# First weight pieces in quarters, gate folds one per unit, block-sum transfers and block sums of x later

## The chip, the cores and the metric

The kernel runs on one core of a Trainium2 chip. The metric is the time of one execution on the device, in microseconds (us). Five engines work side by side: TensorE (PE in the profile, with its weight loads as PEld), VectorE (DVE), ScalarE (ACT), GpSimd (POOL) and SyncE (SP). Here SP only issues DMA transfers; POOL does a little arithmetic and also issues transfers.

## What is computed

The reference is one block of an encoder on 512 positions of 1024 channels, in float32:

```python
h = rmsnorm(x, w)                       # 512 x 1024
parts = h @ w_in                        # one combined projection, 10240 columns
# branch A: Re(2-D DFT) of 4 channel groups, * silu(z_A), linear map to 1024
# branch B, 4 heads of 512 channels:
xc = silu(centred_dwconv(xm, 5 taps) + bias)
q, k = block_diag_proj(xc, ...); v = block_diag_proj(xm, ...)   # blocks of 4 channels
i_pre, f_pre = linear maps of (q, k, v) to one number per head and direction
hh = mlstm(q, k, v, i_pre, log_sigmoid(f_pre))   # forward and backward scans, summed
u = (rmsnorm(sigmoid(o) * hh) + skip * xc) * silu(z_B)          # linear map to 1024
y = sigmoid(g_A) * y_A + sigmoid(g_B) * y_B
out = final_rmsnorm(x + y @ w_out)
```

Three pieces matter here: the projection, the input and forget gates of branch B, which need q, k and v of all heads, and the norm inside u.

## The kernel before

**Products in three.** Every large product is made of three matmuls. `mm3` (L94) splits each operand into a high part, rounded to a shorter format, and a low part, the rest: L96 takes high times high, L97 and L98 the two cross products. `hi_of` (L86) makes high parts on ACT, `lo_of` (L89) low parts on DVE. So each piece of weights costs one step on ACT and one on DVE before TensorE can take it.

**Units.** Weights come in units of 128 x 1024 numbers (512 KB). `fetch` issues a unit's load on SP into one of three raw buffers (L130). `prepare` (L141 to L152) splits it into `whi` and `wlo`, of which there are two buffers each, and issues the next fetch as soon as the raw buffer is free. A unit gives 24 matmuls of 128x512 in `proj`.

**The start.** `load_x` (L203) loads one of eight tiles of x, transposed, and splits it into `hhi` (ACT) and `hlo` (DVE, L206). The first three units are loaded and split in pieces by `load_part` (L209), between the tiles of x: in halves of 512 columns, with the tiles 0 and 4. ACT then squares the tiles of x (L249), DVE adds them (L252), and `norm_rows` (L305) sums over the channels with small matmuls (L309) and makes the norm factor rc; `norm_bcast` (L313) spreads it.

**The loop over units.** One z unit, then 16 x units. The product of each is evacuated and scaled by the norm on DVE (L352) as a tile `sa`; from the fifth on, `conv` (L323) makes one convolved tile `sb` a unit, with four steps on DVE (L331) and two on ACT (L328, L333). At unit 6 `load_gates` (L266) issues six loads of 256 KB with the gate weights, into the tile buffers sa1 to sb3, whose x tiles come later. At unit 10 `fold_gates` (L273) folds the block-diagonal weights into them: for each of the six pieces a multiplication (L282) and a reduction (L283) on DVE. A sum (L285) and a copy make the gate matrix of it. From then on `gate_mm` (L293) multiplies it with the x tiles, one matmul for `sa` and one for `sb` of each (L299), in float32 and with an output of 32 rows; `tile_position` puts four of them in turn on four groups of TensorE's columns. All add up in one accumulator.

**The gates and the heads.** `gate_chain` (L405) copies the accumulator with ACT (L410) and picks rows of it with two small matmuls (L417). Then the four heads follow. Each makes queries, scores (`wf` tiles, cut by POOL's affine selects at L510 and L513), value products (L614, from weights that POOL makes at L494), and products with the output gate (L543 to L545). At the end of a head ACT makes sums of squares (L632), POOL the norm factor `rr` from them (L634, L635), DVE scales by it (L636), and TensorE transposes (L646). ACT scales the convolved tiles by the skip weights (L641).

**Block sums.** The last linear maps use products of block sums in the manner of Strassen. The sums of weight blocks are made in DRAM by 20 jobs: SP copies a block (L158), and POOL adds another to it with an accumulating transfer (L162), which waits for the copy and for earlier sums. The program places the jobs between its stages (`next_job`). SP's transfers are kept in the order of the program, POOL's L162 are not. Sums of blocks of x are made by `block_sums` (L664): four calls, each with two loads on POOL (L668) and work on DVE and ACT, at units 0 to 3 of the first loop behind the heads (L681); at units 6 and 7 of that loop ACT evacuates the products (L697).

**The order of the work.** A scheduler puts the instructions of each engine in order ahead of time, by a model of when each can start. `pin` takes an instruction out of that: it keeps its place of the program among the pinned ones of its engine.

Of the kernel before, what the change touches and what calls it, by code (L numbers as in the profile page):

```python
# [11 lines left out]
ALU = mybir.AluOpType  # L12
# [14 lines left out]
SSQ_AT, RB_AT = (2, 2), (2, 6)  # L27
LOAD_AT, FOLD_AT, CONV_AT, DRAIN_AT = 6, 10, 4, 12
Z_FIRST = 3
# [10 lines left out]
def hybrid_block(ctx: ExitStack, tc, xT, xn, units, blocks, vecs, gates, gbias, consts, dft, fnw, out):  # L40
# [115 lines left out]
    def sum_job(i):  # L156
        if i < 4 * NB:
            pin(nc.sync.dma_start(sums[i // 4, i % 4], blocks[i // 4, (2, 0, 0, 1)[i % 4]], max_dma_last_dim=4 * S * 4))  # L158
        if i > 0:
            b, k = (i - 1) // 4, (i - 1) % 4  # L160
            src = (blocks[b, 3], sums[b, 0], blocks[b, 2], sums[b, 1])[k]
            gp.dma_start(sums[b, k], src, accum_op=ALU.add, max_dma_last_dim=4 * S * 4)  # L162

# [45 lines left out]
    def load_part(i, n):  # L209
        if n == 0:  # L210
            raws[i] = tl("raw", [P, 1024], bufs=NRAW)
            if i < 2:
                items.append((tl("whi", [P, 1024], F32R, bufs=2), tl("wlo", [P, 1024], F32R, bufs=2)))
            else:
                items.append((tl("so0", [P, 1024], F32R), tl("so1", [P, 1024], F32R)))
        hs = slice(n * S, (n + 1) * S)
        nc.sync.dma_start(raws[i][:, hs], units[i][:, hs])
        hi_of(items[i][0][:, hs], raws[i][:, hs])
        lo_of(items[i][1][:, hs], raws[i][:, hs], items[i][0][:, hs])

    state["raw"] = state["split"] = NU0
    for k in range(8):
        load_x(k)
        if k % 4 == 0:
            for i in range(NU0):
                load_part(i, k // 4)
    for i in range(NU0):
# [12 lines left out]
    def wview(name):  # L240
        return vc[:, name : name + 64].rearrange("p (i d) -> p i d", i=16)
# [24 lines left out]
    def load_gates():  # L266
        for n, t in enumerate(("sa1", "sa2", "sa3", "sb1", "sb2", "sb3")):
            j, half = n // 2, n % 2
            grep[j, half] = tl(t, [P, 8, 16, 4])
            src = gates[:, j, 8 * half : 8 * half + 8].rearrange("p i (g d) -> p i g d", d=4)  # L270
            pin(nc.sync.dma_start(grep[j, half], src))

    def fold_gates():  # L273
        folded.append(True)
        folds = [tl("sa0", [P, 2, 16, 16]), tl("sb0", [P, 1, 16, 16])]
        for j, off in enumerate((V_WQ, V_WK, V_WV)):
            dst = folds[j // 2][:, j % 2]
            for half in range(2):
                hs = slice(8 * half, 8 * half + 8)
                g = grep[j, half]  # L280
                w = wview(off)[:, hs].unsqueeze(2).to_broadcast([P, 8, 16, 4])
                ve.tensor_tensor(out=g, in0=g, in1=w, op=ALU.mult)  # L282
                ve.tensor_reduce(out=dst[:, hs, :], in_=g, axis=AX.X, op=ALU.add)  # L283
        f = folds[0]
        ve.tensor_tensor(out=w_gate[0][:, :, 0:16], in0=f[:, 0], in1=f[:, 1], op=ALU.add)  # L285
        se.activation(w_gate[1][:, :, 0:16], folds[1][:, 0], AF.Copy)

# [80 lines left out]
    for n, (kind, i) in enumerate([("z", 0)] + [("x", i) for i in XO]):  # L368
# [17 lines left out]
        if n == LOAD_AT:  # L386
            load_gates()
        if n == FOLD_AT and not folded:
            fold_gates()
        if n >= CONV_AT and ready:  # L390
            conv(ready.pop(0))
        while n >= DRAIN_AT and ready:
            conv(ready.pop(0))
        if folded and len(pending) >= 5:
            gate_mm([pending.pop(0) for _ in range(4)])
# [285 lines left out]
    for q in range(2):  # L681
        accs = [bank("acc") for _ in range(4)]
        for n in range(8):
            if q == 0 and n < 4:
                block_sums(n)
            if q == 1 and n == 2:
# [445 lines left out]
```

## Time and profile before

| | |
|---|---|
| median of 3 runs | 772.92 us (771.41 to 774.53) |
| the profiled execution | 773.64 us |
| its span, first to last instruction | 771.9 us |
| TensorE's granted clock | 0.999 |
| PE busy | 758.5 us (98%) |
| DVE busy | 526.4 us (68%) |
| ACT busy | 411.5 us (53%) |
| POOL busy | 70.5 us (9%) |

The times in the views are counted from the start of the span. In a row of the timeline stand start, duration, engine, line, operation, out<-in, and in brackets how long the engine was idle before it and who ended that. In the view of stretches, each engine's busy time stands with its count of instructions behind it, in the order PE, PEld, DVE, ACT, POOL, then clock, DMA share and GB/s. Matmuls overlap, so a row's duration is longer than the step from one start to the next.

### The profile page before, as it was taken

What the parts mean: (1) busy time and instruction counts of PE and PEld (TensorE: products, weight loads), DVE (VectorE), ACT (ScalarE), POOL (GpSimd) and SP (SyncE); (2) the same over time, 40 slices, a digit from 0 to 9 for tenths busy, and PEclk for the clock granted to TensorE, in tenths of its full rate; (3) what the DMA queues carried; (4) which work ended last, traced back from release to release, by engine and by line L of the source; (5) the groups of instructions that cost most, each with busy time, mean ns of one, the idle gap of its engine ahead of it and who ended that gap; (6) DMA issues with size and microseconds to landing.
All of it is one profiled execution on the core that took longest, in us unless ns stands there. A gap on an engine that the chain in (4) does not pass through costs nothing.

```text
span 771.9 us, 10941 instructions
## 1 busy us (share of the span) xinstructions
PE 758.5 (98%) x4146; PEld 642.1 (83%) x4146; DVE 526.4 (68%) x813; ACT 411.5 (53%) x643; POOL 70.5 (9%) x147
## 2 busy tenths in 40 slices
PE   8999999999999999999999999999999999999996
PEld 7876776788788888888888887899999999988885
DVE  6599876676758574767475693247667678557875
ACT  7434445659446843685463443156544577643444
POOL 0100001011310310031101210000010100000002
PEclk9999999999999999999999999999999999999999
DMA  8348658639460984197403565267654456554452
GB/s 273 105 148 260 190 138 237 173 134 259 97 192 28 289 213 125 43 302 217 120 27 137 141 221 157 86 181 225 192 164 147 135 157 198 179 183 140 147 193 109
DMA packets 40949, 128.55 MB, mean 167 GB/s; under 512 B 4801, under 2 KB 5314, under 8 KB 35778
## 3 DMA queue, kind: packets, MB, share of 16 engines
q1 hardware_dynamic: 37378, 104.80, 40.5%
q0 software_dynamic: 3520, 23.07, 15.2%
q8 instruction: 32, 0.52, 0.3%
q14 instruction: 19, 0.16, 0.1%
HBM read 125.76 MB, written 44.04 MB: 220 GB/s over the span
## 4 chain that ended last, share of the span: by engine, by line
PE 87%; DVE 5%; DMA 3%; ACT 2%; issue 1%; POOL 1%; SPq 0%; POOLq 0%; ACTq 0%
PE acc L96 16%; PE acc L98 16%; PE acc L97 16%; PE wk L98 7%; PE wk L96 7%; PE wk L97 7%; PE acc L544 3%; PE acc L545 3%; PE acc L543 3%; DMA sum<-in_blocks_dram 2%; PE wk L299 1%; PE wk L614 1%; DMA raw<-in_units_dram 1%; DVE t2k L331 1%; DVE wlo L89 1%
## 5 line engine op out<-in xcount | busy, mean ns | idle before, releaser
L89 DVE TENSOR_TENSOR wlo<-raw,whi 128x1024 fp32r<-128x1024 f32 (+1 forms) x105 | 125.4, 1196 | 82.5 <-ACT whi L86 82.4
L86 ACT ACTIVATE whi<-raw 128x1024 fp32r<-128x1024 f32 (+1 forms) x105 | 108.8, 1039 | 128.4 <-PE acc L97 92.0
L96 PE MATMUL acc<-hhi,whi 128*128 128x512 f32 x248 | 97.0, 395 | 2.6 <-ACT whi L86 2.6
L98 PE MATMUL acc<-hhi,wlo 128*128 128x512 f32 x248 | 97.2, 393 | 0.0
L97 PE MATMUL acc<-hlo,whi 128*128 128x512 f32 x248 | 97.0, 391 | 0.0
L96 PEld LDWEIGHTS acc<-hhi,whi 128*128 128x128 f32 x248 | 46.5, 188 | 15.0 <-ACT whi L86 4.8
L98 PEld LDWEIGHTS acc<-hhi,wlo 128*128 128x128 f32 x248 | 46.5, 188 | 14.7 <-DVE sa L352 2.5
L89 DVE TENSOR_TENSOR gwl<-raw,gwh 128x1024 fp32r<-128x1024 f32 (+1 forms) x39 | 47.1, 1208 | 17.0 <-ACT gwh L86 17.0
L86 ACT ACTIVATE gwh<-raw 128x1024 fp32r<-128x1024 f32 (+1 forms) x39 | 40.9, 1048 | 29.7 <-PE acc L97 10.8
L97 PEld LDWEIGHTS acc<-hlo,whi 128*128 128x128 f32 x248 | 46.6, 188 | 10.1 <-DVE hlo L206 0.7
L545 PE MATMUL acc<-whi,hlo 128*128 128x512 f32 x128 | 50.5, 394 | 0.0
L544 PE MATMUL acc<-wlo,hhi 128*128 128x512 f32 x128 | 50.4, 393 | 0.0
L97 PE MATMUL acc<-sb,whi 128*128 128x512 f32 x128 | 50.2, 392 | 0.0
L96 PE MATMUL acc<-sa,whi 128*128 128x512 f32 x128 | 49.8, 390 | 0.3 <-ACT whi L86 0.3
L97 PE MATMUL wk<-vlo,phi 128*128 128x512 f32 x128 | 49.8, 389 | 0.0
L96 PE MATMUL wk<-vhi,phi 128*128 128x512 f32 x128 | 49.6, 390 | 0.0
L98 PE MATMUL acc<-sa,wlo 128*128 128x512 f32 x128 | 49.0, 391 | 0.5 <-DVE wlo L89 0.5
L98 PE MATMUL wk<-vhi,plo 128*128 128x512 f32 x128 | 48.0, 389 | 0.0
L543 PE MATMUL acc<-whi,hhi 128*128 128x512 f32 x128 | 47.6, 392 | 0.0
L331 DVE SCALAR_TENSOR_TENSOR t2k<-sa,vecs,t2k 128x510 f32<-128x510 f32 (+1 forms) x64 | 45.9, 743 | 0.5
L98 PEld LDWEIGHTS acc<-sa,wlo 128*128 128x128 f32 x128 | 24.0, 188 | 5.8 <-DVE wlo L89 1.0
L96 PEld LDWEIGHTS wk<-vhi,phi 128*128 128x128 f32 x128 | 24.0, 188 | 5.7 <-PE acc L417 0.8
(399 smaller groups left out, 1909.4 us busy)
## 6 DMA issues: line engine op xcount, KB each, us to landing
raw<-in_units_dram SPq DMA_DIRECT2D x69, 512.0 KB, 3.9
sum<-in_blocks_dram SPq DMA_DIRECT2D x20, 1024.0 KB, 7.8
raw<-sum SPq DMA_DIRECT2D x64, 256.0 KB, 3.6
raw<-in_blocks_dram SPq DMA_DIRECT2D x48, 256.0 KB, 3.6
sum<-in_blocks_dram POOLq DMA_DIRECT2D x10, 1024.0 KB, 10.9
sum<-sum POOLq DMA_DIRECT2D x10, 1024.0 KB, 9.6
raw<-sum SPq DMA_DIRECT2D x8, 512.0 KB, 4.5
raw<-in_blocks_dram SPq DMA_DIRECT2D x6, 512.0 KB, 4.1
```

Source lines behind the costliest of these rows:

```text
L86: se.activation(dst, src, AF.Copy, scale=scale)
L89: ve.tensor_tensor(out=dst, in0=src, in1=hi.bitcast(F32), op=ALU.subtract)
L96: pin(te.matmul(acc, wh, xh, start=start, stop=False, **skip), pinned)
L97: te.matmul(acc, wh, xl, start=False, stop=False, **skip)
L98: te.matmul(acc, wl, xh, start=False, stop=stop, **skip)
L299: te.matmul(gate_ps[rows, :], w_gate[j][:, i, :], r, start=p < 2, stop=p >= 14, tile_position=(0, 32 * (2 * b + j)))
L331: ve.scalar_tensor_tensor(out=cv[:, o], in0=src[:, s], scalar=cw[k], in1=cv[:, o], op0=ALU.mult, op1=ALU.add)
L543: te.matmul(ops[t], hv(x_hi, k)[:, ts], wh[:, ks], start=k == 0, stop=False)
L544: te.matmul(ops[t], hv(x_hi, k)[:, ts], wl[:, ks], start=False, stop=False)
L545: te.matmul(ops[t], hv(x_lo, k)[:, ts], wh[:, ks], start=False, stop=k == 7)
L614: te.matmul(vp[:, ds], xm[c0 + d][:, b * P : (b + 1) * P], vbf[:, d, :], start=True, stop=True)
```

## The change

Four things are changed, and nothing of what is computed.

1. The first three units come in quarters of 256 columns, with the tiles 0, 2, 4 and 6 of x.
2. The gates are loaded at unit 5 into the buffers vhi0 to vlo2, and folded one piece a unit at units 8 to 13, behind the convolution of that unit; the multiplications are pinned. The gate matmuls can start behind unit 13 instead of behind unit 10.
3. POOL's accumulating transfers are pinned to the order of the program.
4. The block sums of x are made at units 2 to 5 instead of 0 to 3.

```diff
-LOAD_AT, FOLD_AT, CONV_AT, DRAIN_AT = 6, 10, 4, 12
+LOAD_AT, FOLD_AT, CONV_AT, DRAIN_AT = 5, 8, 4, 12
...
-            gp.dma_start(sums[b, k], src, accum_op=ALU.add, max_dma_last_dim=4 * S * 4)
+            pin(gp.dma_start(sums[b, k], src, accum_op=ALU.add, max_dma_last_dim=4 * S * 4))
...
-        hs = slice(n * S, (n + 1) * S)
+        hs = slice(n * 256, (n + 1) * 256)
...
-        if k % 4 == 0:
+        if k % 2 == 0:
             for i in range(NU0):
-                load_part(i, k // 4)
+                load_part(i, k // 2)
...
-        for n, t in enumerate(("sa1", "sa2", "sa3", "sb1", "sb2", "sb3")):
+        for n, t in enumerate(("vhi0", "vlo0", "vhi1", "vlo1", "vhi2", "vlo2")):
...
+    def fold_gates(n):
+        if n == 0:
+            folds.extend([tl("vhi3", [P, 2, 16, 16]), tl("vlo3", [P, 1, 16, 16])])
+        j, half = n // 2, n % 2
+        hs = slice(8 * half, 8 * half + 8)
+        g = grep[j, half]
+        w = wview((V_WQ, V_WK, V_WV)[j])[:, hs].unsqueeze(2).to_broadcast([P, 8, 16, 4])
+        pin(ve.tensor_tensor(out=g, in0=g, in1=w, op=ALU.mult))
+        ve.tensor_reduce(out=folds[j // 2][:, j % 2, hs, :], in_=g, axis=AX.X, op=ALU.add)
+        if n == 5:
+            folded.append(True)
+            f = folds[0]
+            ve.tensor_tensor(out=w_gate[0][:, :, 0:16], in0=f[:, 0], in1=f[:, 1], op=ALU.add)
+            se.activation(w_gate[1][:, :, 0:16], folds[1][:, 0], AF.Copy)
...
-        if n == FOLD_AT and not folded:
-            fold_gates()
...
+        if FOLD_AT <= n < FOLD_AT + 6:
+            fold_gates(n - FOLD_AT)
...
-            if q == 0 and n < 4:
-                block_sums(n)
+            if q == 0 and 2 <= n < 6:
+                block_sums(n - 2)
```

The change moves instructions on every engine. Behind the first places, the changed program's lines are two higher (L299 becomes L301, L641 becomes L643, L410 becomes L412).

On TensorE, near the last x units, before. `sa1` and `sb1` are the second x tile of head 0 and its convolution, `wf0` and `wf1` the two halves of the gate matrix, `wk_47` the accumulator of the gates:

```order
L98 MATMUL acc_184_1006<-hhi3_17_129,wlo_173_956 128x512
L299 MATMUL wk_47_226<-sb1_160_902,wf0_43_217 32x512
L96 MATMUL acc_188_1039<-hhi0_14_126,whi_181_1000 128x512
L97 MATMUL acc_188_1039<-hlo0_18_130,whi_181_1000 128x512
L299 MATMUL wk_47_226<-sa1_158_894,wf1_44_218 32x512
L299 MATMUL wk_47_226<-sb2_169_949,wf0_43_217 32x512
L299 MATMUL wk_47_226<-sa2_167_941,wf1_44_218 32x512
L98 MATMUL acc_188_1039<-hhi0_14_126,wlo_182_1001 128x512
```

After, behind the last x unit:

```order
L98 MATMUL acc_188_1057<-hhi3_17_129,wlo_182_1019 128x512
L301 MATMUL wk_47_244<-sb0_151_847,wf0_43_235 32x512
L301 MATMUL wk_47_244<-sa0_149_839,wf1_44_236 32x512
L301 MATMUL wk_47_244<-sb1_160_904,wf0_43_235 32x512
L301 MATMUL wk_47_244<-sa1_158_896,wf1_44_236 32x512
L301 MATMUL wk_47_244<-sb2_169_959,wf0_43_235 32x512
L301 MATMUL wk_47_244<-sa2_167_951,wf1_44_236 32x512
L301 MATMUL wk_47_244<-sb3_178_1012,wf0_43_235 32x512
L301 MATMUL wk_47_244<-sa3_176_1004,wf1_44_236 32x512
L96 MATMUL wk_198_1108<-phi0_152_849,mhi_196_1103 128x512
```

The 32 gate matmuls stood in batches of 10, 2, 4, 6, 2, 2, 1, 3 and 2 rows; now they stand in three, of 1, 23 and 8, of which the last is shown. Between it and L419, the former L417, are 12 rows, as there were 12 behind the last batch before. On ACT, the four scalings L643 of head 0 now stand one behind the other directly ahead of the copy L412; before, three of the four stood spread over the 18 rows ahead of it.

On DVE, where the folds begin, before. L282 and L283 are the fold, L331 the convolution, L352 the evacuation, L89 the low part of a unit:

```order
L282 TENSOR_TENSOR sa2_88_487<-sa2_88_487,vecs_5_116 128x512
L331 SCALAR_TENSOR_TENSOR t2k_107_579<-sa8_79_442,vecs_5_116,t2k_107_579 128x510
L282 TENSOR_TENSOR sa3_89_489<-sa3_89_489,vecs_5_116 128x512
L331 SCALAR_TENSOR_TENSOR t2k_100_538<-sa7_72_401,vecs_5_116,t2k_100_538 128x511
L282 TENSOR_TENSOR sb1_90_491<-sb1_90_491,vecs_5_116 128x512
L283 TENSOR_REDUCE sa0_121_662<-sa1_87_485 128x128
L282 TENSOR_TENSOR sb2_91_493<-sb2_91_493,vecs_5_116 128x512
L283 TENSOR_REDUCE sa0_121_662<-sa2_88_487 128x128
L352 TENSOR_TENSOR sa9_86_483<-acc_85_458,rb_48_227 128x512
```

After, with the evacuation now at L354, the convolution at L333, and the fold's lines by chance the same:

```order
L282 TENSOR_TENSOR vhi0_80_462<-vhi0_80_462,vecs_5_116 128x512
L354 TENSOR_TENSOR sa10_99_554<-acc_98_529,rb_48_245 128x512
L333 SCALAR_TENSOR_TENSOR t2k_116_643<-sa9_92_513,vecs_5_116,t2k_116_643 128x511
L89 TENSOR_TENSOR wlo_103_565<-raw_90_486,whi_102_564 128x1024
L283 TENSOR_REDUCE vhi3_109_605<-vhi0_80_462 128x128
L333 SCALAR_TENSOR_TENSOR t2k_116_643<-sa9_92_513,vecs_5_116,t2k_116_643 128x511
L333 SCALAR_TENSOR_TENSOR t2k_123_686<-sa10_99_554,vecs_5_116,t2k_123_686 128x510
L354 TENSOR_TENSOR sa11_106_595<-acc_105_570,rb_48_245 128x512
```

Six of nine rows were folds; now one multiplication and one reduction stand to a unit, with the unit's other work between.

On POOL, at the end of head 0, before. `wf` rows are the selects of head 1, `rr` the norm factors of head 0, `sum20` the first sum of block 2:

```order
L510 AFFINE_SELECT wf2_340_1717<-wf2_340_1717 128x128
L162 DMA sum20_84<-in_blocks_dram 128x2048
L513 AFFINE_SELECT wf2_340_1717<-wf2_340_1717 128x128
L510 AFFINE_SELECT wf3_341_1718<-wf3_341_1718 128x128
L513 AFFINE_SELECT wf3_341_1718<-wf3_341_1718 128x128
L634 TENSOR_SCALAR rr_288_1541<-ss_285_1524 128x1
```

After:

```order
L162 DMA sum12_82<-in_blocks_dram 128x2048
L636 TENSOR_SCALAR rr_288_1559<-ss_285_1542 128x1
L637 TENSOR_TENSOR rr_288_1559<-rr_288_1559,mhalf_2_98 128x1
L636 TENSOR_SCALAR rr_291_1579<-ss_285_1542 128x1
L637 TENSOR_TENSOR rr_291_1579<-rr_291_1579,mhalf_2_98 128x1
L636 TENSOR_SCALAR rr_294_1599<-ss_285_1542 128x1
L637 TENSOR_TENSOR rr_294_1599<-rr_294_1599,mhalf_2_98 128x1
L636 TENSOR_SCALAR rr_297_1619<-ss_285_1542 128x1
L637 TENSOR_TENSOR rr_297_1619<-rr_297_1619,mhalf_2_98 128x1
L162 DMA sum11_81<-sum10_80 128x2048
L162 DMA sum13_83<-sum11_81 128x2048
L162 DMA sum20_84<-in_blocks_dram 128x2048
L496 TENSOR_TENSOR mhi_337_1731<-vecs_5_116,consts_31_203 128x512
```

Ahead of the first rr stood sum20; now sum12 stands there, and sum11, sum13 and sum20 have moved behind the last rr, ahead of the value weights of head 1. The same holds of heads 1 and 2 with the next blocks. SP's order is the old one, with six more loads at its start.

More of the change, by code (lines that the diff above doesn't have):

```diff
@@ L271, in load_gates @@
             pin(nc.sync.dma_start(grep[j, half], src))
[L273 to L286, printed above, removed]
+    folds = []
+    def fold_gates(n):
[12 more added lines that the diff above has]
+            se.activation(w_gate[1][:, :, 0:16], folds[1][:, 0], AF.Copy)
     gate_ps = bank("wk")
```

## The prediction

> **What bounds the kernel now.** The page comes first: it says which engine is never idle.
>
> ```profile
> span 771.9 us, 10941 instructions
> PE 758.5 (98%) x4146; PEld 642.1 (83%) x4146; DVE 526.4 (68%) x813; ACT 411.5 (53%) x643; POOL 70.5 (9%) x147
> ```
>
> TensorE is the bound, and it takes its matmuls in a written order. So time can come only from places where its stream is slower than its own pace, or from matmuls that cost more than they must. The timeline of PE gives the pace, and two places where it stands.
>
> ```profile
> 54.35 0.39 PE L96 MATMUL acc<-hhi,whi 128*128 128x512 f32 x1
> 54.58 0.39 PE L97 MATMUL acc<-hlo,whi 128*128 128x512 f32 x1
> 55.46 0.50 PE L96 MATMUL acc<-hhi,whi 128*128 128x512 f32 x1 [0.49 <-ACT whi L86]
> ...
> 60.88 0.39 PE L98 MATMUL acc<-hhi,wlo 128*128 128x512 f32 x1
> 62.18 0.50 PE L96 MATMUL acc<-hhi,whi 128*128 128x512 f32 x1 [0.92 <-ACT whi L86]
> ```
>
> From start to start a 128x512 matmul takes 0.23 us (54.35 to 54.58). A gap costs its start-to-start time less 0.23, since the pipeline has to fill again: 54.58 to 55.46 costs 0.65 us and 60.88 to 62.18 costs 1.07 us, more than the idle time in brackets. I count all losses so. The chain of waits then shows the longest pieces that aren't matmuls at pace:
>
> ```profile
> 67.92 2.70 PE wk L299 x20
> 76.30 0.98 PE wk L299 x4
> 82.95 1.00 PE wk L299 x8
> 94.60 1.84 PE wk L299 x12
> 100.56 0.98 PE wk L299 x4
> 109.26 0.98 PE wk L299 x4
> 120.90 0.98 PE wk L299 x2
> 122.54 0.99 PE wk L299 x6
> 130.55 0.98 PE wk L299 x4
> ...
> 193.90 0.83 POOL sum L162
> ```
>
> The gate matmuls (L299) come in nine batches. Their pieces sum to 11.45 us, and a batch of 2, 4, 6 or 8 instructions takes the same 0.98 to 1.00 us. The last row is a transfer that POOL issued late; that reaches TensorE too, as shown further down. The change touches each of these places.
>
> **Part by part. The gate matmuls.** Each row of the program is two instructions (32 rows, 64 instructions in nine batches). A batch's instructions go to four column groups of the array and run side by side, so the time goes by rounds of four rows. One round costs 0.98 us, two rounds (12 instructions, 6 rows) cost 1.84, three (20, 10 rows) cost 2.70: 0.12 us and 0.86 a round. What lies around a batch is in the timeline of PE:
>
> ```profile
> 67.53 0.39 PE L98 MATMUL acc<-hhi,wlo 128*128 128x512 f32 x1
> ...
> 70.55 0.50 PE L98 MATMUL acc<-hhi,wlo 128*128 128x512 f32 x1
> ```
>
> From the last ordinary matmul before the first batch to the first one behind it are 3.02 us; less 0.23 for that one, 2.79, which is 0.09 over its piece. Nine batches therefore cost 11.45 + 0.81 = 12.26 us. In the changed order there are three, of 1, 23 and 8 rows: 1, 6 and 2 rounds, or 0.98 + 5.28 + 1.84 + 0.27 = 8.37 us. That saves 3.9 us. What if the rounds don't fill as well in the long batch? With one lost round for each half of it the saving is 2.2; if the cost at entry is paid more lightly than I read, it may be 4.3.
>
> **The folds.** Before, twelve instructions of the fold (a multiplication and a reduction for each of six pieces) stand together on DVE. Their price and DVE's load, from the groups of 48 to 64 us and the stretches of 20 us:
>
> ```profile
> L283 DVE TENSOR_REDUCE sa<-sa 128x128 f32<-128x512 f32 x3 | 2.0, 675 | 0.0
> ...
> 40.00:60.00 20.00, 19.51 (x87) 15.69 (x86) 19.65 (x30) 6.97 (x9) 0.00 (x0) 1.00 0.55 187
> 60.00:80.00 20.00, 19.08 (x90) 12.70 (x89) 19.83 (x29) 10.21 (x14) 1.90 (x2) 1.00 0.74 217
> ```
>
> The third figure after the comma is DVE: full for 40 us, 12 x 0.68 = 8 us of it folds. The weight halves (whi on ACT, wlo on DVE) and the evacuations queue behind, ACT waits for the evacuated tile, and the two gaps of 0.65 and 1.07 follow. With one piece a unit DVE gets 1.3 us more in each of six units, and the ordinary work of a unit leaves room for nearly that much. Both gaps should go: -1.7 us. At worst DVE stays full until about 100 us and one gap of about 1.1 remains, -0.6. Behind it nothing is late: the fold is ready some units before the long batch stands in the order. The loads of the gates are issued one unit earlier and read two earlier, three units (16 us) behind their issue; I count nothing for them.
>
> **The end of the gate.** L410 (ACT) copies the finished gate sums for L417, TensorE's next reader. Three of the four scalings of L641 ran earlier before; now all four wait for the last batch and stand ahead of that copy.
>
> ```profile
> 197.59 0.72 ACT L641 ACTIVATE sb<-sb,vecs 128x512 f32<-128x512 f32 x1 [3.91 <-DVE plo L89]
> ```
>
> Four are 2.9 us, with the copy behind them. TensorE has 12 matmuls (2.7 us) between batch and reader, and the batch itself lasts 1.84, in which the first scalings can start. Between 0 and 1.2 us are left over; I take +0.5, about the middle.
>
> **The sums in their order.** Pinning L162 keeps POOL's accumulating transfers where the program writes them, behind the norm factors rr rather than between. Now, in the timeline of all engines:
>
> ```profile
> 196.17 0.39 PE L545 MATMUL acc<-whi,hlo 128*128 128x512 f32 x1
> 196.47 0.49 DVE L636 TENSOR_SCALAR so<-so,rr 128x512 f32<-128x512 f32 x1 [5.08 <-POOL rr L635]
> 197.02 0.55 PE L646 MATMUL wk<-consts,so 128*128 128x128 f32 x3 [0.46 <-DVE so L636]
> 197.63 0.39 PE L544 MATMUL acc<-wlo,hhi 128*128 128x512 f32 x1
> ...
> 198.54 1.04 PE L646 MATMUL wk<-consts,so 128*128 128x128 f32 x5 [0.52 <-DVE so L636]
> ```
>
> POOL issued a transfer at 193.90, when its copy had landed, and three selects and four rr stood behind it; DVE waited 5.08 us for the first rr, and the transposes L646 for DVE. The two gaps cost 0.62 and 0.68 us, and the waits of PE say that there is a third:
>
> ```profile
> PE wk L646 <- DVE so L636: 1.2, 3, 0.5
> ```
>
> 1.2 us of idle time in three waits, so 0.2 in the last, which with its refill is 0.4. Together 1.7, and 1.8 with what the short transposes between lose. In the changed order another sum takes that place, the one that POOL now issues earlier:
>
> ```profile
> 176.11 0.83 POOL L162 DMA_DIRECT2D sum<-in_blocks_dram  x1 [17.05 <-DMA sum<-in_blocks_dram]
> ```
>
> Its copy had landed at 176 us, more than 10 us ahead of the first rr, so rr is no longer held: -1.8 us (-1.2, if the ACT and DVE steps that rr feeds are late too, to -2.3). POOL then stands some 10 us in the chain of accumulations behind rr, and the next head's value weights (L494) behind that; TensorE reads these only in the value products (L614), behind the next head's scores. SP's queue keeps its order.
>
> **Quarters at the start.** Six halves become twelve quarters: six more loads, ACT splits and DVE splits. Rows by shape, for 512 and 256 columns, ACT first, then DVE; then the last x tile on DVE and the weight loads behind these:
>
> ```profile
> L86 ACT ACTIVATE whi<-raw 128x512 fp32r<-128x512 f32 x4 | 2.4, 623 | 1.4 <-DMA raw<-in_units_dram 1.3
> ...
> L455 ACT ACTIVATE half_r<-half 128x256 fp32r<-128x256 f32 x1 | 0.4, 415 | 0.0
> ...
> L89 DVE TENSOR_TENSOR wlo<-raw,whi 128x512 fp32r<-128x512 f32 x4 | 2.7, 687 | 1.7 <-ACT whi L86 1.7
> ...
> L260 DVE TENSOR_TENSOR em_r<-a_col,vecs 128x256 f32<-128x256 f32 x1 | 0.4, 417 | 0.0
> ...
> 18.77 0.74 DVE L206 SCALAR_TENSOR_TENSOR hlo<-vlo,vecs,hhi 128x512 fp32r<-128x512 f32 x1
> ...
> L130 SPq DMA_DIRECT2D raw<-in_units_dram x5: 327/328/328, 14.5 to 23.6; - x5
> ```
>
> ACT's idle 1.3 us in the first of these rows, before the second unit's half, stops TensorE about as long, and a quarter should land in time to fill most of it. But TensorE doesn't keep what it gains: its last matmuls on x need the low half of the last x tile, which DVE ends at 19.51, and DVE stands in one unbroken row of work up to there from its first steps on the second x tile. Twelve quarters cost DVE 12 x 0.42 - 6 x 0.69 = 0.9 us more by these rows, ACT 12 x 0.415 - 6 x 0.623 = 1.2; some overlap between instructions takes it to about 0.6 and 0.9. DVE also starts about half a microsecond sooner. I take +0.3 us, from -0.5 (the gain kept) to +1.5 (both engines' extra work, end to end). The weight buffers of these units come free only after their last quarters, about 18 us, not the 14.5 of the last row; the next load then lands 3.9 us later (its median in the DMA issues, below), near 22, and TensorE wants that unit at about 25, after 1.1 us on ACT and 1.2 on DVE. There is about a microsecond to spare.
>
> **The block sums of x.** They move two units on, away from the two units behind head 3. Their loads and ACT's evacuations L697 still meet at one place:
>
> ```profile
> 463.68 0.39 PE L98 MATMUL acc<-sa,wlo 128*128 128x512 f32 x1
> ...
> 465.61 0.50 PE L98 MATMUL acc<-sa,wlo 128*128 128x512 f32 x1 [0.53 <-DVE wlo L89]
> ```
>
> 1.93 us for three steps of 0.23 is a loss of 1.2. ACT evacuates an accumulator ahead of the next weight split there, in both orders, so I count 0, from -1.2 to +1.0 (the sums' work now falls nearer to that place).
>
> **Sum.** +0.3 - 3.9 - 1.7 + 0.5 - 1.8 + 0 = -6.6 us. The profiled execution took 773.64 us (1.7 around its span), 0.72 above the median of the runs, 772.92. So 767.0 for that execution, and against the median 766.3 us, 0.9% faster. A difference of 0.5%, 3.9 us, is about what a measurement of this kernel can tell from none.
>
> **Rivals.** *The folds' cover is too thin (0.12).* TensorE, with fewer pauses, meets a DVE that is just full: for it speak the two stretches above, against it that DVE falls off behind 80 us. Then the two gaps stay and one like the longer comes on top: -6.6 + 1.7 + 1.1, 769.1 us, on the bound of no change.
>
> *The long batch isn't cheaper (0.08).* Rounds of four are seen only up to three rounds. At 2.2 saved and the end of the gate at its worst (+1.2): 768.7; if the long batch fell to two rows a round, its 12 rounds would take 5.2 us more and the time would be 771.5.
>
> *The start costs its worst (0.08):* +1.5, 767.5, and if the first whole unit is also 1 us late, 768.5. [...]
>
> *The block sums' gap goes (0.06):* -1.2, 765.1.
>
> *Slower (0.04): loads starved by chained sums.* With the pins three accumulating transfers follow each other behind rr in the first heads.
>
> ```profile
> raw<-in_units_dram SPq DMA_DIRECT2D x69, 512.0 KB, 3.9
> ...
> sum<-in_blocks_dram POOLq DMA_DIRECT2D x10, 1024.0 KB, 10.9
> ```
>
> If a weight load had to wait for all three (33 us) while three raw buffers cover about 16 us (24 matmuls, 5.4 us, a unit), TensorE would stand 17 us once: 783 us. It decides from the moment that a load takes more than 16 us; 3.9 us today, with sums under way at times, speaks against it.
>
> **Chances.** The forecast has 0.62. The bound of no change is 769.1 us, so a tenth of the forecast, where several terms end badly at once, and half of the first three rivals fall within it: faster 0.74, same 0.22, slower 0.04. The range: low is the sum with every term at its better end, -0.5 - 4.3 - 1.7 - 2.3 - 1.2, about 763.0; high takes in the first three rivals up to where two of them meet, 770.5.
>
> **What would show it.** Right: three groups of gate matmuls with a long one of about 5.3 us; no waits for whi at 54 and 61 us; no wait of DVE for rr in the first head; L646 without gaps. Wrong: a batch of 23 rows over 6 us; whi gaps between 70 and 110 us; a wait of L417 over 1.2 us; the last x tile on DVE later than 21 us; a weight load of over 10 us beside the sums.

## The result and the profile after

The changed kernel takes 765.65 us (median of 5 runs, 765.20 to 766.53), against 772.92 before: a ratio of 0.9909, with a 95% interval from 0.9892 to 0.9926. The forecast was 766.3. The profiled execution took 766.53 us, with a span of 764.4; so between the two profiled executions 7.1 us went. The page first:

```profile
span 764.4 us, 10960 instructions
PE 753.4 (99%) x4146; PEld 643.3 (84%) x4146; DVE 525.3 (69%) x819; ACT 410.9 (54%) x649; POOL 70.2 (9%) x147
```

The same matmuls take a shorter span. PE is busy 5.1 us less, though no matmul was taken out: the gate matmuls now share their time better. The chain of waits between 80 and 126 us shows them:

```profile
88.30 0.98 PE wk L301 x2
111.72 5.28 PE wk L301 x46
117.00 0.43 PE acc L98
122.25 1.85 PE wk L301 x16
124.80 1.31 ACT sb L643 x2
```

Three batches of 2, 46 and 16 instructions take 0.98, 5.28 and 1.85 us, 8.11 in all; nine took 11.43. Behind each stands an ordinary matmul that starts late: the 0.43 of L98 against a pace of 0.23 is a part of what a batch costs at its borders. The last row is the end of the gate, where two scalings and the copy behind them are still to come. What TensorE waits for, by the waits of PE (two rows that are the same in both kernels are left out):

```profile
...
PE acc L98 <- DVE wlo L89: 0.8, 2, 0.5
PE acc L96 <- ACT so L86: 0.7, 1, 0.7
PE acc L97 <- DVE hlo L206: 0.5, 1, 0.5
...
PE acc L96 <- ACT whi L86: 0.3, 1, 0.3
PE wk L96 <- ACT t2k L412: 0.2, 1, 0.2
```

Before, TensorE waited 2.9 us in four waits for whi. The two in the middle of the x units (0.49 and 0.92) are gone; the one at the start, 1.23, has become one of 0.72 for so; and the one of 0.28 behind head 3 is still there. Those of L646 for DVE are gone too. New are two more at the start, for hlo and one of the two for wlo, and the one for L412. DVE in the stretches of 40 to 60 and 60 to 80 us:

```profile
40.00:60.00 20.00, 20.00 (x90) 16.57 (x89) 20.00 (x29) 9.07 (x13) 0.00 (x0) 1.00 0.58 198
60.00:80.00 20.00, 20.00 (x90) 16.54 (x89) 19.18 (x28) 9.14 (x11) 1.90 (x2) 1.00 0.76 215
```

DVE is as full as it was (20.00 and 19.18 us), yet PE is busy all the time. So it is not the load of DVE that stopped TensorE, but what stood ahead in its order. Before, the timelines of DVE and ACT have

```profile
52.87 0.68 DVE L352 TENSOR_TENSOR sa<-acc,rb 128x512 f32<-128x512 f32 x1
53.64 0.82 ACT L328 ACTIVATE t2k<-sa,vecs 128x512 f32<-128x512 f32 x1 [3.69 <-DVE sa L352]
54.37 1.04 ACT L86 ACTIVATE whi<-raw 128x1024 fp32r<-128x1024 f32 x1
```

The evacuation L352 stood behind the folds on DVE, the convolution's step L328 waited 3.69 us for it on ACT, and the split of the next weights stood behind that step. After, the split at 55.47 us waits 0.72 us on ACT, only until TensorE frees its buffer. At the end of head 0, in the timeline of POOL first:

```profile
184.91 0.82 POOL L162 DMA_DIRECT2D sum<-in_blocks_dram  x1
185.86 0.19 POOL L636 TENSOR_SCALAR rr<-ss 128x1 f32<-128x1 f32 x1
```

Then in that of DVE:

```profile
186.74 0.49 DVE L638 TENSOR_SCALAR so<-so,rr 128x512 f32<-128x512 f32 x1 [0.44 <-POOL rr L637]
```

And of PE:

```profile
191.31 0.49 PE L648 MATMUL wk<-consts,so 128*128 128x128 f32 x3
```

The transfer ahead of rr has no wait in brackets, DVE waits 0.44 instead of 5.08 us, and the transposes start without a gap. The one loss is the start. The timeline of ACT has

```profile
7.85 0.42 ACT L86 ACTIVATE so<-raw 128x256 fp32r<-128x256 f32 x1 [1.60 <-DMA raw<-in_units_dram]
8.47 0.72 ACT L86 ACTIVATE hhi<-vhi,vecs 128x512 fp32r<-128x512 f32 x1 [0.21 <-DMA vhi<-in_xT_dram]
```

that of DVE the last x tile,

```profile
19.90 0.75 DVE L206 SCALAR_TENSOR_TENSOR hlo<-vlo,vecs,hhi 128x512 fp32r<-128x512 f32 x1
```

that of PE the product which waits for it,

```profile
20.70 0.50 PE L97 MATMUL acc<-hlo,whi 128*128 128x512 f32 x1 [0.46 <-DVE hlo L206]
```

and the DMA issues of the weight tile, from SP's queue, with the issue times behind the three durations,

```profile
L130 SPq DMA_DIRECT2D raw<-in_units_dram x5: 327/328/377, 19.0 to 26.1; - x5
```

ACT is idle for 1.60 us where it was for 1.34; the second x tile comes at 8.47, hardly earlier than the 8.55 before; and the last x tile is done on DVE at 20.65 us, 1.14 later than 19.51. DVE's work on the second x tile, before and after, begins at

```profile
9.31 0.75 DVE L206 SCALAR_TENSOR_TENSOR hlo<-vhi,vecs,hhi 128x512 fp32r<-128x512 f32 x1
9.23 0.75 DVE L206 SCALAR_TENSOR_TENSOR hlo<-vhi,vecs,hhi 128x512 fp32r<-128x512 f32 x1 [0.51 <-ACT hhi L86]
```

From there to the last x tile are 9.46 us before (to 18.77) and 10.67 after (to 19.90): 1.21 longer, less 0.08 for the earlier begin. The next weight load is issued at 19.0 instead of 14.5, later than I thought, and no wait of TensorE shows for it.

### The profile page after: what moved, and what is told of

The parts are those of the page before. It is cut to its first block, busy times and chain, and to the rows that moved or that the text cites. A ratio compares the mean times of both kernels' runs of the same rounds, so it can differ in the third digit from the quotient of the medians.

```text
span 764.4 us, 10960 instructions
## 1 busy us (share of the span) xinstructions
PE 753.4 (99%) x4146; PEld 643.3 (84%) x4146; DVE 525.3 (69%) x819; ACT 410.9 (54%) x649; POOL 70.2 (9%) x147
## 4 chain that ended last, share of the span: by engine, by line
PE 93%; ACT 2%; DVE 2%; issue 1%; DMA 1%; POOL 0%; SPq 0%; POOLq 0%; DVEq 0%; ACTq 0%
PE acc L96 17%; PE acc L98 17%; PE acc L97 16%; PE wk L96 7%; PE wk L97 7%; PE wk L98 7%; PE acc L546 3%; PE acc L545 3%; PE acc L547 3%; PE wk L616 2%; PE wk L301 1%; PE acc L987 1%; PE acc L985 1%; PE acc L986 1%; PE wk L648 1%
## 5 line engine op out<-in xcount | busy, mean ns | idle before, releaser
L86 ACT ACTIVATE whi<-raw 128x1024 fp32r<-128x1024 f32 (+2 forms) x109 | 109.4, 1008 | 139.8 <-PE acc L97 89.6
L89 DVE TENSOR_TENSOR wlo<-raw,whi 128x1024 fp32r<-128x1024 f32 (+2 forms) x109 | 126.0, 1159 | 77.3 <-ACT whi L86 77.2
L98 PE MATMUL acc<-hhi,wlo 128*128 128x512 f32 x248 | 96.7, 391 | 0.2 <-DVE wlo L89 0.2
L89 DVE TENSOR_TENSOR gwl<-raw,gwh 128x1024 fp32r<-128x1024 f32 (+1 forms) x39 | 47.1, 1209 | 18.8 <-ACT gwh L86 18.8
L98 PEld LDWEIGHTS acc<-hhi,wlo 128*128 128x128 f32 x248 | 46.6, 188 | 11.1 <-DVE t2k L333 0.8
L98 PE MATMUL acc<-sa,wlo 128*128 128x512 f32 x128 | 49.0, 391 | 0.5 <-DVE wlo L89 0.5
L98 PE MATMUL wk<-vhi,plo 128*128 128x512 f32 x128 | 48.0, 389 | 0.0
L333 DVE SCALAR_TENSOR_TENSOR t2k<-sa,vecs,t2k 128x510 f32<-128x510 f32 (+1 forms) x64 | 45.3, 749 | 0.0
L96 PEld LDWEIGHTS acc<-sa,whi 128*128 128x128 f32 x128 | 24.0, 188 | 6.1 <-ACT whi L86 1.2
L98 PEld LDWEIGHTS acc<-sa,wlo 128*128 128x128 f32 x128 | 24.0, 188 | 5.8 <-DVE wlo L89 1.0
```

Of the source, the lines that this page charges most:

```text
L86: se.activation(dst, src, AF.Copy, scale=scale)
L89: ve.tensor_tensor(out=dst, in0=src, in1=hi.bitcast(F32), op=ALU.subtract)
L96: pin(te.matmul(acc, wh, xh, start=start, stop=False, **skip), pinned)
L98: te.matmul(acc, wl, xh, start=False, stop=stop, **skip)
L333: ve.scalar_tensor_tensor(out=cv[:, o], in0=src[:, s], scalar=cw[k], in1=cv[:, o], op0=ALU.mult, op1=ALU.add)
```

## The experiments

**The start: halves, and transfers against instructions.** Three kernels take the quarters apart. The first has the halves of before:

```diff
-        hs = slice(n * 256, (n + 1) * 256)
+        hs = slice(n * S, (n + 1) * S)
...
-        if k % 2 == 0:
+        if k % 4 == 0:
...
-                load_part(i, k // 2)
+                load_part(i, k // 4)
```

> The changed kernel with the first units in halves again, all else kept. Theory: in the changed kernel's trace the start is 1.15 us late (the long group of norm matmuls begins at 21.74 us, before it was 20.60), since the second x tile lands no earlier although less is loaded ahead of it, and nine quarters instead of three halves are left for ACT behind it. Undone, that group begins at about 20.6 and the whole run is about 1.1 us faster than the changed kernel: 764.5 us. Rival, the forecast's own size (+0.3): 765.3. Second rival, no cost at all: 765.6.

Measured: 765.14 us (765.08 to 765.65), 765.10 in the profiled execution, 1.43 less than the changed kernel's. In the chain the long group of norm matmuls stands at

```profile
20.60 1.46 PE wk L311 x14
```

against 20.76 in the chain before the change and 21.91 in the changed kernel's. So the loss of 1.15 us at the start is the quarters' doing. The medians differ by only 0.5 us, nearer to the rival's 765.3, and these few runs hardly tell that from nothing; the place in the trace does tell it. All the traces agree on where it arises. The norm matmuls stand 1.99 to 2.01 us behind DVE's step on the last x tile in each of them. That step comes 9.46 or 9.47 us behind DVE's step on the second x tile in all six kernels with halves at the old places, and 10.67 or 10.68 in all four with quarters.

The second loads halves and splits each as two quarters:

```diff
-        nc.sync.dma_start(raws[i][:, hs], units[i][:, hs])
+        if n % 2 == 0:
+            ls = slice(n * 256, (n + 2) * 256)
+            nc.sync.dma_start(raws[i][:, ls], units[i][:, ls])
```

> The changed kernel with the first units loaded in halves at the old places, but split in quarters, two in a row. It tells the cost of the instructions from that of the transfers. If the twelve smaller instructions are the cost: ACT and DVE each lose about 0.1 us for each of six extra ones, three of which stand behind the second x tile; the norm matmuls begin 0.3 to 0.6 us later than in halves, at 20.9 to 21.2. If the transfers and the work that they put off are the cost: at 20.6 to 20.9, most of the 1.15 us gone.

Measured: 765.40 us (764.77 to 766.02). The second x tile in the timeline of ACT:

```profile
8.16 0.72 ACT L86 ACTIVATE hhi<-vhi,vecs 128x512 fp32r<-128x512 f32 x1
```

The norm matmuls in the chain:

```profile
20.58 1.46 PE wk L313 x14
```

The norm matmuls are where they were with halves, but not because the extra instructions are free. The second x tile came 0.22 us sooner here than in the first kernel (8.16 against 8.38; with halves it varies from 8.12 to 8.88 between the traces), and the row of work on DVE behind it takes 9.67 us, 0.21 more than the 9.46 with halves. So six quarters behind that tile in place of three halves cost 0.21 us, and a load that happened to land sooner hid it. The changed kernel has nine quarters there, 4.5 halves' worth of work. A half takes 0.60 us on DVE from start to start and a quarter 0.34. So of its 1.21 us some 0.9 is work that the quarters put off until behind the second x tile, and 0.3 is the price of smaller pieces.

The third kernel has it the other way round, two loads of a quarter and one split of a half:

```diff
+        hs = slice(n * S, (n + 1) * S)
+        for q in range(2):
+            ls = slice((2 * n + q) * 256, (2 * n + q + 1) * 256)
+            nc.sync.dma_start(raws[i][:, ls], units[i][:, ls])
...
-        if k % 2 == 0:
+        if k % 4 == 0:
...
```

> The changed kernel with the first units loaded in quarters, two in a row at the halves' old places, and split in halves: the same bytes ahead of each x tile as before the change, in twice as many transfers. If smaller transfers are slower, the second x tile lands later than before the change (8.5 us) by 0.3 us or more and the norm matmuls begin after 20.9. If only the bytes count, both stand where they stood: 8.5 and 20.6.

Measured: 766.23 us (765.92 to 767.86). The timeline of ACT:

```profile
9.19 0.72 ACT L86 ACTIVATE hhi<-vhi,vecs 128x512 fp32r<-128x512 f32 x1 [1.02 <-DMA vhi<-in_xT_dram]
```

The chain:

```profile
21.40 1.46 PE wk L313 x14
```

With the same bytes ahead of it the second x tile comes 0.8 to 1.0 us later than in the two kernels above (8.38 and 8.16), ACT waits for it, and the norm matmuls are 0.8 us late. I took the smaller transfers for the cause. The timeline of SP shows another one. First the kernel with halves, then this one:

```profile
1.70 1.39 SPq L217 DMA_DIRECT2D raw<-in_units_dram  x3
3.13 1.38 SPq L204 DMA_DIRECT2D vhi<-in_xT_dram  x3
...
1.71 2.81 SPq L219 DMA_DIRECT2D raw<-in_units_dram  x6
4.56 1.38 SPq L204 DMA_DIRECT2D vhi<-in_xT_dram  x3
```

Each of these issues takes SP 0.48 us from start to start, for 128 KB as for 256 KB (1.43 us for three, 2.85 for six). Three more of them stand ahead of the second x tile here, so its load is issued 1.43 us later. From issue to landing it takes 4.6 us, less than the 5.3 in the changed kernel. The changed kernel has three issues ahead of it, as the kernel before had, and issues it at 3.13 us like that one. So the third experiment shows a price of more loads, but not the cause of the changed kernel's loss. What the size of a transfer costs was not shown: by the DMA view of the first 9 us, loads of 128 KB took a median of 3.5 us from issue to landing here and 5.2 in the changed kernel, those of 256 KB 5.4 in the kernel with halves.

**Gate batches alone.** The kernel before, its gate matmuls held back to four batches of 8 rows; nothing else of the change:

```diff
-        if folded and len(pending) >= 5:
+        if folded and n >= 13 and len(pending) >= 5:
...
-                    te.matmul(gate_ps[rows, :], ...)
+                    pin(te.matmul(gate_ps[rows, :], ...))
```

> The kernel before with nothing changed but the places of its gate matmuls: they are held to four batches of 8 rows; the folds stay in one burst. Theory: the cost goes by rounds of four rows and by batches, four times 1.84 us plus about 0.2 at its borders, 8.2 us instead of 13.2; the two gaps for whi at 54 and 61 us stay (1.7 us). The run is 5.0 us faster than before: 767.9 us. Rival, that the gain came from the spread folds alone: 772.9. If rounds can't be filled beyond what was seen, 769 to 770.

Measured: 768.18 us (767.35 to 769.18), a ratio of 0.9938 (0.9923 to 0.9953). The chain has four batches of 1.85 us, of which here is the first:

```profile
89.03 1.85 PE wk L299 x16
```

The timeline of PE still has the two gaps, with the idle time in brackets:

```profile
55.31 0.50 PE L96 MATMUL acc<-hhi,whi 128*128 128x512 f32 x1 [0.47 <-ACT whi L86]
...
61.99 0.50 PE L96 MATMUL acc<-hhi,whi 128*128 128x512 f32 x1 [0.92 <-ACT whi L86]
```

So the batches alone bring about 4.9 us without touching the two gaps, and these are a part of their own. The 4.9 is not all the batches': in this profile the waits of L646 for DVE come to 0.4 us instead of 1.2, since the head is earlier against the copies, and the end of the gate costs about 0.4 more.

**The pins undone.** The changed kernel without them:

```diff
-            pin(gp.dma_start(sums[b, k], src, accum_op=ALU.add, max_dma_last_dim=4 * S * 4))
+            gp.dma_start(sums[b, k], src, accum_op=ALU.add, max_dma_last_dim=4 * S * 4)
```

> The changed kernel with POOL's accumulating transfers left to the scheduler again; its order on POOL around the first head is then the one before the change. Theory: POOL waits for the copy of sum20 ahead of the first rr again, DVE waits about 5 us for rr, the transposes L648 show gaps that sum to about 2.1 us, and the run takes 767.7 us. Rival: with the rest of the change everything up to the head is 7 us earlier or later against the copies, so that the copy lands in time and nothing is lost: 765.7.

Measured: 768.37 us, and a wide spread, 766.35 to 770.26; the four above span 0.6 to 1.9. The kernel of the next experiment, which keeps the pins, took 765.59 on the same chip. In the profiled execution (770.26), by the timeline of POOL:

```profile
190.58 0.83 POOL L162 DMA_DIRECT2D sum<-in_blocks_dram  x1 [6.20 <-DMA sum<-in_blocks_dram]
```

By that of DVE:

```profile
193.17 0.49 DVE L638 TENSOR_SCALAR so<-so,rr 128x512 f32<-128x512 f32 x1 [6.25 <-POOL rr L637]
```

And of PE:

```profile
193.71 0.55 PE L648 MATMUL wk<-consts,so 128*128 128x128 f32 x3 [1.62 <-DVE so L638]
```

The wait is back, longer than it was: the head is 4.5 us earlier than before the change, and the copy lands only 3.3 us earlier (POOL issues behind it at 190.58 instead of 193.90). The first gap alone is 1.8 us instead of 0.6. How long it lasts hangs on when a transfer lands, which would explain the spread; no second profile of this kernel shows it. The profiled execution is the slowest of the six, and some 1.4 us of it are not the pins': between 22 and 26 us TensorE's granted clock is 0.57 (its mean over the span is 0.996), and matmuls there follow each other in 0.43 us instead of 0.23. No other kept trace has that there.

**The block sums of x back at units 0 to 3:**

```diff
-            if q == 0 and 2 <= n < 6:
-                block_sums(n - 2)
+            if q == 0 and n < 4:
+                block_sums(n)
```

> The changed kernel with the block sums of x at units 0 to 3 again. Theory: they are off TensorE's path in both places; the gap of 1.1 us near 456 us stays, since there two weight buffers are held by matmuls that stand last in the order of TensorE, whoever works on the sums. The small gap of 0.23 us near 446 us, new in the changed kernel, goes: 765.4 us. Rival: the later place is worth something that the gaps don't show: 766 to 767.

Measured: 765.59 us (765.12 to 766.03), no difference that could be measured. The small gap near 446 us is gone; the large one is where it was:

```profile
456.56 0.50 PE L96 MATMUL acc<-sa,whi 128*128 128x512 f32 x1 [0.28 <-ACT whi L86]
...
457.83 0.51 PE L98 MATMUL acc<-sa,wlo 128*128 128x512 f32 x1 [0.53 <-DVE wlo L89]
```

**Rounds, not rows.** The kernel of the first experiment with the two gate matmuls of a tile exchanged, so that the early single row joins the long batch:

```diff
-                for j, r in enumerate((xc[i], xm[i])):
+                for j, r in ((1, xm[i]), (0, xc[i])):
```

> The kernel in halves of the first experiment, with the two gate matmuls of a tile written in the other order, the one with the second half of the gate matrix first. That half is ready last, so the single early row joins the long batch: 24 and 8 rows, 6 and 2 rounds, instead of 1, 23 and 8. By rounds (0.86 us each) and batches (0.12 in it and 0.2 around it) 1.2 us less than in the first experiment: 763.9 us, with a batch of 24 rows in 5.3 us. If the cost went by rows, nothing would change: 765.1.

Measured: 763.88 us (763.12 to 763.96), and the chain has

```profile
108.95 5.29 PE wk L301 x48
...
119.49 1.85 PE wk L301 x16
```

24 rows take what 23 took, and one batch with its round and its borders, 0.98 and about 0.2 us, is gone.

**The gap behind head 3.** The same kernel, with the last two units of the first product loop in a written order (`part` issues the products of one unit with the operand tiles named, `merge` is L697; all three matmuls of each product are pinned there):

```diff
...
+                part(w6, 0, 6, range(12, 15))
+                part(w6, 1, 6, range(12, 15))
+                part(w7, 2, 7, range(12, 15))
+                part(w6, 0, 6, (15,))
+                part(w6, 1, 6, (15,))
+                merge(0)
+                merge(1)
+                unit()
+                part(w7, 3, 7, range(12, 15))
+                part(w7, 2, 7, (15,))
+                part(w7, 3, 7, (15,))
...
```

> The kernel of the experiment with the swapped gate matmuls, and in it the last two units of the first product loop written out in an order of their own and pinned: the matmuls with the last operand tile of the first unit come ahead of the rest of the second, so that one weight buffer is free 15 matmuls earlier, and its evacuations stand ahead of the rest too. Theory: the gaps near 455 us (0.44 and 0.70, with their refills about 1.3 us) come from that buffer and go: 762.6 us. Rival, that the sums of x or ACT's other work hold the next weights: 763.9, the gaps where they were.

Measured: 762.14 us (762.01 to 762.23), the lowest median of all, a ratio of 0.9863 (0.9842 to 0.9884) to before. The timeline of ACT shows the next weights split at once, behind the first evacuation and ahead of the second. They are ready at 450.97, over 2 us before TensorE takes them, at 453.29:

```profile
449.41 0.60 ACT L700 ACTIVATE yb<-acc 128x512 f32<-128x512 f32 x1 [2.06 <-PE acc L98]
449.91 1.06 ACT L86 ACTIVATE whi<-raw 128x1024 fp32r<-128x1024 f32 x1
```

Of the gaps of 0.44 and 0.70 us (from start to start, less 0.23) 0.19 is left, for the low half of the weights, which stands on DVE behind a step of the block sums. So the cause was TensorE's own order, which did its last products on the first of the two units late. That order holds two things, the weight buffer and the accumulator whose evacuation stands ahead of the split on ACT. The experiment frees both at once, so it doesn't show which of them held the split.

**The folds in a burst again.** The changed kernel with the loads and folds of before and the gate matmuls held as in the fourth experiment:

```diff
-LOAD_AT, FOLD_AT, CONV_AT, DRAIN_AT = 5, 8, 4, 12
+LOAD_AT, FOLD_AT, CONV_AT, DRAIN_AT = 6, 10, 4, 12
...
-        if FOLD_AT <= n < FOLD_AT + 6:
-            fold_gates(n - FOLD_AT)
+        if n == FOLD_AT and not folded:
+            fold_gates()
...
```

> The changed kernel with its folds in one burst again (loads at unit 6, folds at unit 10, old buffers) and its gate matmuls held to four batches of 8 rows: 8 rounds and four batches, by their rows 0.5 us cheaper than the changed kernel's 1, 23 and 8. It tells what the spread of the folds alone is worth. Theory: the two gaps for whi near 55 and 62 us come back, 0.65 and 1.07 us and 0.2 of refills; 765.65 - 0.5 + 1.9 = 767.1 us. Rival: the gaps came from the many small gate batches or from the sums; then none comes back and the run takes 765.2.

Measured: 769.79 us (768.46 to 773.25), more than any theory said. A part of that is the chip: the kernel before took 773.81 there, 0.9 more than in the first comparison, and the ratio is 0.9957 (0.9935 to 0.9979). The span of the profiled execution is 767.5, 3.1 more than the changed kernel's. The waits of PE, with the total, the number and the longest:

```profile
PE acc L96 <- ACT whi L86: 2.0, 4, 0.9
PE wk L96 <- ACT t2k L410: 1.6, 1, 1.6
PE acc L98 <- DVE wlo L89: 1.1, 2, 0.8
```

Against the changed kernel that is 1.7 us more for whi, 1.4 for the copy of L410 and 0.3 for wlo, 3.4 in all; with 0.5 less for the gate batches and 0.2 more for refills that is the 3.1. The two gaps of whi came back as the theory has it. The second row was in no expectation: here the last gate batch stands six rows further down in TensorE's order, and TensorE, which needs the bank that this copy reads for its next product, has less work of its own behind the batch while ACT goes through the four scalings:

```profile
129.34 0.51 PE L96 MATMUL wk<-phi,mhi 128*128 128x512 f32 x1 [1.61 <-ACT t2k L410]
```

**Three tries for a faster one.** First the kernel with the written order, and the third unit's halves behind the next x tile:

```diff
-        if k % 4 == 0:
-            for i in range(NU0):
-                load_part(i, k // 4)
+        for i in ((0, 1), (2,), (), ())[k % 4]:
+            load_part(i, k // 4)
```

> The fastest kernel so far (halves, swapped gate matmuls, last units of the product loop reordered; 762.1 us) with one step in the start moved: the halves of the third unit are loaded and split behind the next x tile instead of ahead of it. If the chain of ACT splits behind the second x tile sets the start, that tile lands up to 0.66 us earlier, the two small gaps (0.39 and 0.21 us) go and it gains 0.3 to 0.6: 761.6 us. If TensorE has too little to do without the third unit, a gap opens near 8 us instead and the time is 762.1 or more.

Measured: 762.20 us (761.30 to 763.33). The start did what was meant: the x tile stands on ACT at 7.36 us instead of the 8.48 of the kernel that it changes, the norm matmuls at 20.18 instead of 20.69. But the gap of 0.19 us at 453 us has grown to 1.3, in the timeline of PE:

```profile
454.54 0.50 PE L98 MATMUL acc<-sa,wlo 128*128 128x512 f32 x1 [1.15 <-DVE wlo L89]
```

Ahead of it in that of DVE:

```profile
452.14 0.75 DVE L670 SCALAR_TENSOR_TENSOR xr<-xr,vecs,rb 128x512 f32<-128x512 f32 x1 [3.53 <-DMA xr<-in_xT_dram]
```

The low half of the weights stands behind a step of the block sums that waits for its load of x, 3.53 us here and 2.41 in the kernel that this one changes. Why the load came later is open. So I put the block sums back at units 0 to 3, first without the moved loads and then with them:

```diff
-            if q == 0 and 2 <= n < 6:
-                block_sums(n - 2)
+            if q == 0 and n < 4:
+                block_sums(n)
```

> The fastest kernel so far (halves, swapped gate matmuls, last units of the product loop reordered; 762.1 us), with the block sums of x at units 0 to 3 again. In the kernel with the moved load of the third unit a gap of 1.3 us opened at 453 us, where DVE waited 3.5 us for a late load of x for the sums and the low part of the next weights stood behind it. Theory: with the sums two units earlier that load isn't in the way, the gap (0.19 us here) goes, and it runs in 761.9 us, without the spread that a load just in time brings. Rival: the earlier sums hold up something else between 425 and 445 us: 762.5 or more.

> The same with the halves of the third unit behind the next x tile. Theory: the start keeps its gain of 0.5 us, and the gap of 1.3 us at 453 us, which took it away, is gone with the earlier sums: 761.4 us. Rival: the gap has another cause and stays: 762.2.

Measured: 763.22 us (763.00 to 763.39) and 762.35 (762.04 to 763.15). Both theories fell. In the first of them, by the timeline of all engines:

```profile
452.47 1.22 DVE L89 TENSOR_TENSOR tl<-xs,th 128x1024 fp32r<-128x1024 f32 x1
...
453.94 1.22 DVE L89 TENSOR_TENSOR wlo<-raw,whi 128x1024 fp32r<-128x1024 f32 x1
...
455.21 0.51 PE L98 MATMUL acc<-sa,wlo 128*128 128x512 f32 x1 [0.40 <-DVE wlo L89]
```

Now other steps of the sums stand ahead of the low half of the weights. This trace also lost 0.4 us at the start (the norm matmuls at 21.09 instead of 20.69), with the very same loads there, so starts vary by that much. In the second the gain at the start was gone as well, with the norm matmuls at 21.06; the waits of PE have

```profile
PE acc L96 <- ACT whi L86: 1.8, 2, 1.5
```

and the longer of the two is at the start, for the second unit's half. Which of the four is the fastest is not settled. Against the kernel before on their own chips the ratios are 0.9863 for the written order alone, 0.9852 (0.9834 to 0.9870) with the moved loads, 0.9867 (0.9852 to 0.9882) with the earlier sums and 0.9855 (0.9836 to 0.9873) with both: the intervals overlap. What the traces show is that neither edit closes more gaps than it opens; the profiled spans are 759.9, 760.6, 761.5 and 761.4 us.

## Why the prediction held, point by point

The sum was right to 0.7 us, as -6.6 was forecast and -7.3 measured between the medians. That it came so near is in part luck: three gains were about 1.1 us larger than forecast, and the start cost 0.85 us more.

- *The gate matmuls*: forecast -3.9. The pieces came out as they were worked out (0.98, 5.28 and 1.85 us; the nine before sum to 11.43, a slip of 0.02 in the prediction). I had missed that the second step behind a batch loses another 0.11 us (it is 0.34 instead of 0.23), at six batches 0.7; the gain is nearer to 4.5. The batches alone brought 4.9 us in a kernel with four of them, where the rows of before fill 12 rounds and eight are left, and one batch and one round less brought 1.2. Rounds of four are shown up to six in a batch.
- *The folds*: forecast -1.7; both gaps went, with their refills (0.11 us each, a step of 0.34 instead of 0.23) 1.9, and came back with the burst. The reason was half right. I let DVE be full, and asked whether spreading leaves it room. It is full in both kernels. What counts is that the evacuation, and by it the split of the next unit on ACT, no longer stands behind a row of folds.
- *The end of the gate*: +0.5 forecast, 0.4 measured. It isn't L417 that waits, as I had said, but a product shortly ahead of it, which takes the bank that the copy of L410 (now L412) reads. The kernel with the burst, where that wait was 1.61, shows that my upper end of 1.2 was too low in general.
- *The sums in their order*: -1.8 forecast, 2.1 us of gaps gone. Without the pins the loss is larger than before the change.
- *The quarters*: +0.3 forecast, +1.15 measured, inside the bounds but the step that failed. I took ACT and DVE to start on the second x tile about half a microsecond sooner, since a quarter should land sooner than a half. The third quarter landed no sooner than a half does (ACT took it at 7.85 us, and 7.74 with halves), and DVE began 0.08 us sooner. Among the four traces with quarters there is one where the tile stands on ACT at 7.44, so it can come sooner; why it mostly doesn't is open. And I had counted only the extra instructions, +0.6, but no work put off: three of six halves stood behind that tile, now nine of twelve quarters do. That work is about 0.9 of the 1.21 us, and smaller pieces are the other 0.3, half of what I had put down. In a row of work two quarters cost DVE 0.67 us and a half 0.60: that price of smaller pieces is the smaller part of the loss.
- *The block sums of x*: 0 forecast, 0 measured. That ACT's order makes the gap there, as I had it, falls short: ACT still evacuates ahead of the split in the kernel with the written order, and the gap is nearly gone. TensorE's order of the last matmuls makes it.
- *The rivals*: the third, a start at its worst, came true to three quarters of its price. DVE's cover held and the long batch was as cheap as the short. Loads were not starved by the sums, though around 200 us they are slower: in the DMA view of 195 to 235 us four loads have a median of 7.3 us to landing, against 5.3 in the same stretch before. Single ones took up to 12.0 us between 140 and 330 us, more than the 10 that I had named as a sign of being wrong. But before the change it was up to 13.6, so that sign told nothing, and all are under 16.

## What to carry to other kernels

Count what a bounding engine loses from start to start, with the refill behind each break (here 0.11 us), and look first at how often its stream is broken: here 32 rows of short matmuls cost 0.86 us less for each round that was saved, and about 0.3 for each batch. Where a busy engine delays the one that sets the time, its order may be the cause and not its load: between 40 and 80 us DVE was busy for 39.5 us before and for 39.2 after, and the two gaps of TensorE there went. A smaller first piece brought nothing here, since it arrived no sooner (ACT took it at 7.85 us, the half at 7.74), and the work that it put off came behind (about 0.9 of 1.21 us). Count the issues ahead of a load as well as the bytes: each took SP 0.48 us here.

## What the runs showed of the hardware

Matmuls of 32 output rows on four column groups ran side by side, four instructions starting within 0.02 us (111.65 to 111.67 in the changed kernel): six rounds of up to four in 5.28 us, 0.86 a round, in float32. An interrupted stream of TensorE paid about 0.2 us around each batch of them, 0.09 ahead and 0.11 at the second step behind. No run ties the 0.2 us to a cause. The 0.11 stands also behind a wait, with no batch ahead of it: in the kernel before, the step behind the gap at 55.46 us is 0.34 us, as behind a batch, instead of 0.23.

Between 1.7 and 4.6 us an issue took SP 0.48 us from start to start, whether it loads 128 or 256 KB. Six loads of 128 KB ahead of a transfer instead of three of 256 KB, with the same bytes, put its issue off by 1.43 us, and the step that waits for it by 0.8 to 1.0.

In a row of work DVE took 0.60 us from start to start for a split of 512 columns and 0.34 for one of 256.
